# Hybrid encoder layer on one core: the mixers' weights split during the first feed-forward and kept in DRAM

## The chip, the core and the metric

One core of a Trainium2 chip runs the whole layer. The metric is the device time of one execution in microseconds; the median of three runs before the change is 1479.0 us (1477.66 to 1479.29).

## What is computed

One layer, on a prompt of 512 rows and a sample of 256 rows of width 1024, all in float32 (`rms_norm` scales by the root mean square of a row and by a gain):

```python
def encoder_layer(x, ...):
    x = x + 0.5 * swiglu(rms_norm(x, g_ffn1), w_ffn1_gu, w_ffn1_down)
    proj = rms_norm(x, g_mix) @ w_in            # 1024 x 3072
    a_q, a_k, a_v, b_q, b_k, b_v = split(proj)  # 512 columns each
    # mixer A: 8 heads x 64, dilated windows; mixer B: 4 heads, difference of two softmaxes
    # q and k: rms_norm per head, then rotary; outputs: rms_norm per head
    x = x + concat(norm(o_a), norm(o_b)) @ w_out  # 1024 x 1024
    x = x + 0.5 * swiglu(rms_norm(x, g_ffn2), w_ffn2_gu, w_ffn2_down)
    return rms_norm(x, g_final)
# swiglu: silu(g) * u @ w_down, g and u = halves of x @ w_gu, hidden width 2816
```

## The kernel before

**Precision.** Every float32 product is made of three: an operand is split into hi (rounded by a cast on ScalarE, ACT) and lo (the rest, a subtract on VectorE, DVE, or GpSimd, POOL), and hi x hi, hi x lo and lo x hi are summed in PSUM. A weight tile has both parts side by side and is 4 KB a partition for 128 x 512 values. `split3` (lines 253 to 256) makes this pair.

**Stages.** The first feed-forward (`f1`, about 31 to 534 us), the mixers (about 533 to 861 us), the output product through `w_out` (about 860 to 947 us) and the second feed-forward (`f2`). The 768 rows are six tiles of 128. 

**Feed-forward.** The hidden width is 22 chunks of 128. A chunk's gate and up products use seven products instead of eight by sums of weight blocks (Strassen's scheme as Winograd arranged it): POOL makes the sums S1 to S4, ACT and DVE split seven weight tiles. Chunks come in groups (3, 3, 3, 3, 3, 2, 2, 3); after each group but the last, its down products run, into six PSUM banks, one a row tile, in `contract` (line 148), first for column half 0, then for half 1. `run` (line 373) lists steps of two functions, a preparation (loads and splits) and a run (matmuls and evictions); the preparation is traced `AHEAD = 3` steps before its run. With the first two chunks done in `begin`, `f1` has 20 x 7 product steps, 19 x 2 down steps, 6 preparations for the last group, 6 row tiles and one step of its own for the rotary tables, 191 in all. Weight pairs live in `ws` (6 buffers), raw tiles in `sf` (3) and `blk`.

**Order.** The program is traced in this order, and a scheduler that works with modelled times then fixes each engine's instruction order; each engine, and the SP queue that issues nearly all DMAs, runs strictly in it.

**Mixers.** Eight units: 0 to 3 are mixer B's heads, 4 to 7 pairs of mixer A's heads. Twelve `quantum` slots a unit project it from the normalized rows: half a row tile each, 12 matmuls of 384 columns with `ws` as the moving operand (line 644). `rotary` normalizes q and k (r_z is a step of the root, line 84), rotates them on POOL (lines 668, 669) and DVE (line 675, qd); `scores`, `transposed` (line 745, pT) and `values` (line 761) are attention, 13 slots behind. A unit's weights come in four pieces kk of 256 rows x 384 columns: `load_piece` (line 612) loads a raw tile in two DMAs, casts it on ACT (line 620) and subtracts on POOL (line 621) into one of five `ws` buffers. Piece 0 is asked for five slots ahead, pieces 1 and 2 one slot ahead, piece 3 at the unit's first slot. `raw` has two buffers. Mixed outputs of units 0 to 5 go to DRAM (`mT_dram`, line 813).

**Output product.** From slot 98, `early_out` multiplies the mixed tiles 0 to 5 (`mTs`, fetched back by `mixed_split`, line 866, through the same `raw` buffers) with 24 pieces of `w_out` (`early_piece`, line 872: load, ACT cast, POOL subtract). Units 6 and 7 follow with four pieces that `f2.half` (line 272) loads and splits.

Of the kernel before, what the change touches and what calls it, by code (L numbers as in the profile page):

```python
# [10 lines left out]
F32 = mybir.dt.float32  # L11
F32R = mybir.dt.float32r
# [23 lines left out]
def encoder_layer(ctx: ExitStack, tc: tile.TileContext, a, y_prompt, y_sample):  # L36
    nc = tc.nc
    V, S, G, T = nc.vector, nc.scalar, nc.gpsimd, nc.tensor
    dma = nc.sync.dma_start
# [4 lines left out]
    dpool = ctx.enter_context(tc.tile_pool(name="dram", bufs=1, space=bass.MemoryType.DRAM))  # L44
# [27 lines left out]
    xp = XPool()  # L72
# [180 lines left out]
    def split3(dst, src, lo=V):  # L253
        hi = S.copy(dst[:, 0], src)  # L254
        lo.tensor_tensor(dst[:, 1], src, dst[:, 0].bitcast(F32), op=ALU.subtract)  # L255
        return hi

    class FeedForward:
# [111 lines left out]
                for k, t in enumerate(self.tmp):  # L370
                    split3(self.B[nm][k], t[:, slot])

        def run(self, tail, aside=None):

            steps = []
            act = self.act
# [148 lines left out]
        V.tensor_scalar(gcol[:, 28:29], gcol[:, 28:29], 1.0 - LAMBDA_INIT, None, op0=ALU.mult)  # L525


    tabs = tc.alloc_tile_pool(name="tabs", bufs=1, reuse_waits="tile")
    with tile_pool(name="h1", bufs=12) as h1, tile_pool(name="b1", bufs=7) as b1, tile_pool(name="w1", bufs=6) as w1:
        made = []  # L530

        def hb1(name):
            n = len(made)
            if n < 16:
                if n % 2 == 0:
                    made.append(hpool.tile([P, 2, 2, HALF], F32R, tag="blk", name=name))
# [16 lines left out]
        f1.begin(lambda: three_rows((3, 4, 5), third, "n1b", (V, V, None)), lambda: rows_between((0, 1, 2), third, "n1a"),  # L553
                 True)
        hT2 = []

        def post1(t, n):
            if n == 0:
                if len(later) >= 3:
                    run_later()  # L560
                return
            if t == 0:
                roots_table()
                hT2.extend(hpool.tile([P, 2, NTOK], F32R, tag="blk", name=f"hTb{k}") for k in range(KT))
# [18 lines left out]
    with tile_pool(name="w2", bufs=5) as w2, tile_pool(name="mix", bufs=2) as mp:  # L583
        nbias = mp.tile([P, 896], F32, tag="nbias", name="nbias", bufs=1)
        dma(nbias, a["nbias"])

        lst = w2.tile([P, 768], F32, tag="raw", name="lam_st", bufs=2)
        l4 = lst[:, 0:256].rearrange("p (a b d) -> p a b d", b=2, d=64)
        for i, nm in enumerate(("lam_q1", "lam_k1", "lam_q2", "lam_k2")):
            dma(l4[:, i // 2, i % 2, :], row_of(nm))  # L590
# [9 lines left out]
        state = {}  # L600
# [9 lines left out]
            return bass.AP(ap.tensor, ap.offset + step, [*outer, (-step, two), inner])  # L610

        def load_piece(u, kk):
            base = 0 if is_a(u) else 1536
            w3 = w_in[:, base:base + 1536].rearrange("(k p) (s c) -> p k s c", p=P, s=3)
            raw = w2.tile([P, 2, 3, P], F32, tag="raw", name=f"wi{u}_raw{kk}", bufs=2)
            for e in range(2):
                dma(raw[:, e], w3[:, kk * 2 + e, :, (u % 4) * P:(u % 4 + 1) * P])
            s = w2.tile([P, 2, 2, 384], F32R, tag="ws", name=f"wi{u}_ws{kk}", bufs=5)
            rr = raw.rearrange("p k s c -> p k (s c)")
            S.copy(s[:, 0], rr)  # L620
            G.tensor_tensor(s[:, 1], rr, s[:, 0].bitcast(F32), op=ALU.subtract)  # L621
# [113 lines left out]
        def transposed(u, si, m, qt):  # L735
            nt = SEQS[si][1]
            nm = f"a{u}s{si}_{m}{qt}"
            pt = state["sm", u, si, m if is_a(u) else 0, qt]
            e = qt % 2
            if e == 0:  # L740
                state["pT", u, si, m, qt // 2] = mp.tile([P, 2, nt, 256], F32R, tag="pT", name=f"{nm}_pT")
            dst = state["pT", u, si, m, qt // 2]
            ps = bank([P, nt, P], f"{nm}_tp")
            for k in range(nt):
                T.transpose(ps[:, k, :], pt[:, k * P:(k + 1) * P], ident)
            split(dst[:, 0, :, e * P:(e + 1) * P], dst[:, 1, :, e * P:(e + 1) * P], ps)
# [81 lines left out]
        for u in range(8):  # L828
# [4 lines left out]
            n = s0  # L833
# [30 lines left out]
        early = {}  # L864

        def mixed_split(u):
            raw = w2.tile([P, NTOK], F32, tag="raw", name=f"mTraw{u}", bufs=2)
            dma(raw, mT_dram[u])
            mTs[u] = hpool.tile([P, 2, NTOK], F32R, tag="blk", name=f"mTs{u}")
            split(mTs[u][:, 0], mTs[u][:, 1], raw)  # L870

        def early_piece(c, n):
            raw = w2.tile([P, 512], F32, tag="raw", name=f"eo{c}{n}_raw", bufs=2)
            dma(raw, w_out[rows_of(c), n * 512:(n + 1) * 512])
            ws = w2.tile([P, 2, 512], F32R, tag="ws", name=f"eo{c}{n}_ws", bufs=5)
# [16 lines left out]
        for i in range(24):  # L892
            c, n, g = i % 6, i // 6 % 2, i // 12
# [11 lines left out]
    with tile_pool(name="h3", bufs=28) as h3, tile_pool(name="w3", bufs=6) as w3:  # L905
        wt3 = w_tiles(w3)
        f2 = FeedForward("f2", a["w_ffn2_gu"], a["w_ffn2_down"], 16,
                         lambda name: h3.tile([P, 2, HALF], F32R, tag="hb", name=name),
                         lambda shape, dtype, name: hpool.tile(shape, dtype, tag="blk", name=name), wt3,
                         (4, 4, 4, 4, 3, 3))  # L910
        third = lambda name: wt3([P, D], F32, "gf", name)


        wo = {(c, n): f2.half(w_out, (c + 4) % 8, n, f"wo{c}{n}") for c in (6, 7) for n in range(2)}
        for tiles in ((3, 4, 5), (0, 1, 2)):
            for t in tiles:
                for n in range(2):
# [78 lines left out]
```

## Time and profile before

| | |
|---|---|
| median of three runs | 1479.0 us (1477.66 to 1479.29) |
| the profiled execution: its own time | 1477.56 us |
| its span, first to last instruction | 1475.7 us |
| PE (matmul) busy | 1441.2 us |
| DVE, ACT, POOL busy | 1080.0, 675.5, 441.9 us |
| DMA moved | 103.06 MB |

A busy PE is not PE at its peak, since matmuls are pipelined; where it idles, the wait views name the engine that ended the idle time. [...] Instructions are named out<-in by the program's tile names with the numbers left out, after line and engine; SPq is the SP queue's issue of a DMA. Times are us from the span's start.

### The profile page before, as it was taken

The numbers are of one execution on the slowest core, as the hardware profiler recorded it, in microseconds if no ns is written. First come the engines' busy times: TensorE is split into PE (matmuls) and PEld (weight loads), VectorE is DVE, ScalarE is ACT, GpSimd is POOL, SyncE is SP. The second block draws the span as 40 slices with busy tenths as digits, with TensorE's granted clock in tenths as the row PEclk, the third lists the DMA queues.
The fourth block names the chain that finished last, engine by engine and source line by source line (L and its number), as shares of the span: only waits on it lengthen the run. The fifth ranks groups of instructions, "written<-read, shape, count | busy, mean of one in ns | idle before, by whom it ended". The sixth has DMA issues, their size and how long they took to land.

```text
span 1475.7 us, 21779 instructions
## 1 busy us (share of the span) xinstructions
PE 1441.2 (98%) x8041; PEld 1349.7 (91%) x8041; DVE 1080.0 (73%) x1983; ACT 675.5 (46%) x1471; POOL 441.9 (30%) x323
## 2 busy tenths in 40 slices
PE   6999999999999999999999999999999999999997
PEld 6989999998999999999999987899898999989895
DVE  6867676676777777888887885797584865847586
ACT  6423233332333466666677775553241332414245
POOL 3253213131223224443433234232232312222222
PEclk9999999999999999999999999999999999999999
DMA  4322121213221211111111034123132131312212
GB/s 143 104 64 86 43 87 43 86 46 98 83 75 43 80 56 44 51 47 54 55 47 41 30 101 140 53 72 100 43 94 64 44 100 44 100 58 63 81 43 86
DMA packets 141667, 103.06 MB, mean 70 GB/s; under 512 B 7133, under 2 KB 122618, under 8 KB 141562
## 3 DMA queue, kind: packets, MB, share of 16 engines
q1 hardware_dynamic: 141504, 101.67, 22.4%
q8 instruction: 63, 1.03, 0.3%
q14 instruction: 42, 0.34, 0.1%
q10 hardware_dynamic: 58, 0.01, 0.0%
HBM read 96.16 MB, written 5.51 MB: 69 GB/s over the span
## 4 chain that ended last, share of the span: by engine, by line
PE 76%; DVE 10%; ACT 4%; DMA 3%; POOL 3%; issue 2%; SPq 0%; POOLq 0%; ACTq 0%; DVEq 0%
PE f_p L198 40%; PE f_n0t L148 11%; PE f_n1t L148 11%; PE f L311 3%; DMA wi_raw<-in_w_in 1%; DMA eo_raw<-in_w_out 1%; PE u6s0b_pj L644 1%; PE u7s0b_pj L644 1%; POOL wi_ws L621 1%; POOL eo_ws L877 1%; PE f_y L148 1%; DVE x L153 1%; DVE hTb L122 1%; PE eo_t5n L148 1%; PE eo_t4n L148 1%
## 5 line engine op out<-in xcount | busy, mean ns | idle before, releaser
L198 PE MATMUL f_p<-f_bT,f_wS 128*128 128x384 f32 x1440 | 257.4, 335 | 0.0
L198 PEld LDWEIGHTS f_p<-f_bT,f_wS 128*128 128x128 f32 x1440 | 251.5, 188 | 0.0
L254 ACT CAST f_wS<-f_S 128x512 fp32r<-128x512 f32 x160 | 99.2, 621 | 299.4 <-PE f_n1t L148 125.4
L176 POOL TENSOR_TENSOR f_S<-f_raw,f_S 128x512 f32<-128x512 f32 x40 | 62.3, 1558 | 405.1 <-DVE f_wS L255 405.1
L198 PE MATMUL f_p<-f_b,f_wA 128*128 128x384 f32 x960 | 173.1, 335 | 0.0
L198 PEld LDWEIGHTS f_p<-f_b,f_wA 128*128 128x128 f32 x960 | 167.4, 188 | 1.0
L255 DVE TENSOR_TENSOR f_wS<-f_S,f_wS 128x512 fp32r<-128x512 f32 x160 | 124.1, 791 | 57.2 <-ACT f_wS L254 57.2
L148 PE MATMUL f_n0t<-f_d_ws,f_act 128*128 128x512 f32 x684 | 159.9, 392 | 0.0
L148 PE MATMUL f_n1t<-f_d_ws,f_act 128*128 128x512 f32 x684 | 159.6, 392 | 0.0
L148 PEld LDWEIGHTS f_n1t<-f_d_ws,f_act 128*128 128x128 f32 x684 | 128.3, 188 | 29.0
L148 PEld LDWEIGHTS f_n0t<-f_d_ws,f_act 128*128 128x128 f32 x684 | 128.1, 188 | 28.3
L255 DVE TENSOR_TENSOR f_wA<-f_raw,f_wA 128x512 fp32r<-128x512 f32 x136 | 115.8, 871 | 29.3 <-ACT f_wA L254 29.0
L254 ACT CAST f_wA<-f_raw 128x512 fp32r<-128x512 f32 x136 | 82.1, 620 | 73.2 <-PE f_n0t L148 58.2
L176 POOL TENSOR_TENSOR f_S<-f_raw 128x512 f32<-128x512 f32 x40 | 55.8, 1396 | 161.0 <-DVE f_d_ws L255 127.7
L254 ACT CAST f_d_ws<-f_d_raw 128x512 fp32r<-128x512 f32 x88 | 54.7, 622 | 101.9 <-PE f_p L198 60.4
L198 PE MATMUL f_p<-f_bT,f_wA 128*128 128x384 f32 x480 | 90.5, 335 | 0.0
L198 PE MATMUL f_p<-f_b,f_wS 128*128 128x384 f32 x480 | 90.2, 335 | 0.0
L206 DVE TENSOR_TENSOR f_ev<-f_p,f_u 128x384 f32<-128x384 f32 x120 | 66.5, 554 | 31.5 <-PE f_p L198 31.4
L198 PEld LDWEIGHTS f_p<-f_bT,f_wA 128*128 128x128 f32 x480 | 84.3, 188 | 0.0
L198 PEld LDWEIGHTS f_p<-f_b,f_wS 128*128 128x128 f32 x480 | 84.1, 188 | 0.0
L255 DVE TENSOR_TENSOR f_d_ws<-f_d_raw,f_d_ws 128x512 fp32r<-128x512 f32 x88 | 62.7, 713 | 26.5 <-ACT f_d_ws L254 21.8
L621 POOL TENSOR_TENSOR wi_ws<-wi_raw,wi_ws 128x768 fp32r<-128x768 f32 x32 | 58.9, 1848 | 59.0 <-ACT wi_ws L620 56.6
(911 smaller groups left out, 2783.4 us busy)
## 6 DMA issues: line engine op xcount, KB each, us to landing
f_raw<-in_w_ffn_gu SPq DMA_DIRECT2D x88, 512.0 KB, 3.9
f_d_raw<-in_w_ffn_down SPq DMA_DIRECT2D x88, 256.0 KB, 3.0
wi_raw<-in_w_in SPq DMA_DIRECT2D x64, 192.0 KB, 2.6
eo_raw<-in_w_out SPq DMA_DIRECT2D x24, 256.0 KB, 2.6
mTraw<-mT_dram SPq DMA_DIRECT2D x6, 384.0 KB, 2.9
x<-in_x_prompt SPq DMA_DIRECT2D x4, 512.0 KB, 5.8
y_prompt<-nf_o SPq DMA_DIRECT2D x8, 256.0 KB, 2.3
x<-in_x_sample SPq DMA_DIRECT2D x2, 512.0 KB, 5.4
```

The lines of the kernel that those rows point to most:

```text
L122: V.scalar_tensor_tensor(lo, ps[:, k - k0], gc, hi.bitcast(F32), op0=ALU.mult, op1=ALU.subtract)
L148: T.matmul(ps, lhs[:, ll, t * P:(t + 1) * P], ws[:, rl, off:off + cols], start=(first and ll == 0 and rl == 0), stop=(last and ll == 1))
L153: V.scalar_tensor_tensor(xs, ps, scale, xs, op0=ALU.mult, op1=ALU.add)
L176: G.tensor_tensor(q[nm], q[x], q[y], op=op)
L198: T.matmul(ps, w[:, wl, k * P:(k + 1) * P], self.ff.B[bn][k][:, xl, :], start=(k == 0 and wl == 0 and xl == 0), stop=(k == HK - 1 and wl = ...
L206: V.tensor_tensor(dst, self.ps[nm], other, op=ALU.add)
L254: hi = S.copy(dst[:, 0], src)
L255: lo.tensor_tensor(dst[:, 1], src, dst[:, 0].bitcast(F32), op=ALU.subtract)
L311: T.matmul(p, w[:, wl, k * P:(k + 1) * P], self.B[bn[j]][k][:, xl, :], start=(j == 0 and k == 0 and wl == 0 and xl == 0), stop=(j == 1 and ...
L621: G.tensor_tensor(s[:, 1], rr, s[:, 0].bitcast(F32), op=ALU.subtract)
L644: T.matmul(ps, hT2[k][:, xl, tok:tok + P], w[:, wl, k % 2, :], start=(k == 0 and xl == 0 and wl == 0), stop=(k == KT - 1 and xl == 1))
L877: G.tensor_tensor(ws[:, 1], raw, ws[:, 0].bitcast(F32), op=ALU.subtract)
```

## The change

During `f1`'s run, all of `w_in` (48 pieces of 128 x 512) and `w_out` (16 such pieces) are loaded, split by `split3` (ACT cast, DVE subtract) and stored to DRAM tiles `wi_dram` and `wo_dram`, in which a row of 4 KB holds hi and lo of one partition. The store of a piece is issued together with the next piece's split. The raw tile uses the single `junk` buffer, the pair one of the two `xn` buffers. The steps are inserted into the list of `run`; they have no preparation.

In the mixers `load_piece` issues four DMAs straight into `ws` (hi and lo, two blocks of 128 rows each); `early_piece` and the four last pieces of `w_out` issue one DMA. Cast and subtract go. `raw` has one buffer instead of two, `pT` three instead of two.

```diff
+    def fetch_ahead(i):
+        waiting["raw"] = xp.tile([P, 512], F32, "junk", f"sa{i}_raw")
+        dma(waiting["raw"], pieces[i][0])
+    def split_ahead(i):
+        if "ws" in waiting:
+            ws, dst = waiting.pop("ws")
+            dma(dst, ws.bitcast(F32))
+        if i < len(pieces):
+            ws = xp.tile([P, 2, 512], F32R, "xn", f"sa{i}_ws")
+            split3(ws, waiting["raw"])
+            waiting["ws"] = ws, pieces[i][1]
+    ahead = [e for i in range(len(pieces)) for e in ((i + 0.3, lambda i=i: fetch_ahead(i)),
+                                                     (i + 1.0, lambda i=i: split_ahead(i)))]
+    ahead.append((len(pieces) + 1.0, lambda: split_ahead(len(pieces))))
...
+            if spread:
+                rate = (len(steps) - 30) / spread[-1][0]
+                for when, fn in reversed(spread):
+                    steps.insert(6 + int(when * rate), (lambda: None, fn))
...
-        f1.run(post1, prepare)
+        f1.run(post1, prepare, ahead)
...
         def load_piece(u, kk):
-            raw = w2.tile([P, 2, 3, P], F32, tag="raw", name=f"wi{u}_raw{kk}", bufs=2)
+            s = w2.tile([P, 2, 2, 384], F32R, tag="ws", name=f"wi{u}_ws{kk}", bufs=5)
+            c = u % 4 * P
             for e in range(2):
-                dma(raw[:, e], w3[:, kk * 2 + e, :, (u % 4) * P:(u % 4 + 1) * P])
-            s = w2.tile([P, 2, 2, 384], F32R, tag="ws", name=f"wi{u}_ws{kk}", bufs=5)
-            S.copy(s[:, 0], rr)
-            G.tensor_tensor(s[:, 1], rr, s[:, 0].bitcast(F32), op=ALU.subtract)
+                for l in range(2):
+                    dma(s[:, l, e].bitcast(F32).rearrange("p (s c) -> p s c", c=P),
+                        wi_dram[u // 4, kk * 2 + e, :, :, l, c:c + P].rearrange("s p c -> p s c"))
...
-                state["pT", u, si, m, qt // 2] = mp.tile([P, 2, nt, 256], F32R, tag="pT", name=f"{nm}_pT")
+                state["pT", u, si, m, qt // 2] = mp.tile([P, 2, nt, 256], F32R, tag="pT", name=f"{nm}_pT", bufs=3)
...
-            raw = w2.tile([P, NTOK], F32, tag="raw", name=f"mTraw{u}", bufs=2)
+            raw = w2.tile([P, NTOK], F32, tag="raw", name=f"mTraw{u}", bufs=1)
...
         def early_piece(c, n):
-            raw = w2.tile([P, 512], F32, tag="raw", name=f"eo{c}{n}_raw", bufs=2)
-            dma(raw, w_out[rows_of(c), n * 512:(n + 1) * 512])
             ws = w2.tile([P, 2, 512], F32R, tag="ws", name=f"eo{c}{n}_ws", bufs=5)
-            S.copy(ws[:, 0], raw)
-            G.tensor_tensor(ws[:, 1], raw, ws[:, 0].bitcast(F32), op=ALU.subtract)
+            dma(ws.bitcast(F32), wo_dram[(c + 4) % 8, n])
...
-        wo = {(c, n): f2.half(w_out, (c + 4) % 8, n, f"wo{c}{n}") for c in (6, 7) for n in range(2)}
+                wo[c, n] = wt3([P, 2, 512], F32R, "ws", f"wo{c}{n}")
+                dma(wo[c, n].bitcast(F32), wo_dram[(c + 4) % 8, n])
```

## Rows read from the trace of the kernel before

**Rows 1.** The page, busy time of each engine (share of span, instructions).

```profile
PE 1441.2 (98%) x8041; PEld 1349.7 (91%) x8041; DVE 1080.0 (73%) x1983; ACT 675.5 (46%) x1471; POOL 441.9 (30%) x323
```

**Rows 2.** Busy times by stretch: length, PE, PEld, DVE, ACT, POOL, clock, DMA, GB/s.

```profile
95.87:139.90 44.03, 44.03 (x253) 44.03 (x253) 34.98 (x51) 18.15 (x32) 11.65 (x9) 1.00 0.28 84
139.90:164.42 24.52, 24.52 (x109) 20.27 (x109) 13.48 (x19) 4.56 (x7) 6.17 (x5) 1.00 0.15 43
...
618.00:659.00 41.00, 39.59 (x271) 38.96 (x270) 35.08 (x90) 27.28 (x78) 16.05 (x10) 1.00 0.16 49
...
741.00:782.00 41.00, 41.00 (x289) 40.44 (x288) 33.13 (x89) 30.23 (x81) 14.84 (x10) 1.00 0.16 49
```

**Rows 3.** PE's waits, 577 to 741 us: who for whom, total us, times, longest.

```profile
PE a0s_o L761 <- DVE a1s_p L733: 1.4, 1, 1.4
PE a1s_o L761 <- DVE a2s_p L733: 1.4, 1, 1.4
PE a2s_o L761 <- DVE a3s_p L733: 1.3, 1, 1.3
PE a3s_o L761 <- ACT a3s_pT L90: 0.7, 1, 0.7
```

**Rows 4.** Timeline (start, length, engine, line) of DVE and POOL in units 2 to 4.

```profile
618.23 0.15 DVE L84 TENSOR_TENSOR u2s0b_r_z<-u2s0b_r_y 128x8 f32<-128x8 f32 x1
...
643.95 1.84 POOL L621 TENSOR_TENSOR wi_ws<-wi_raw,wi_ws 128x768 fp32r<-128x768 f32 x1 [2.31 <-ACT wi_ws L620]
644.46 1.35 DVE L84 TENSOR_TENSOR u2s1b_r_z<-u2s1b_r_y 128x8 f32<-128x8 f32 x1
...
647.76 2.32 DVE L675 TENSOR_TENSOR u2s1b_qd<-u2s1b_qn,tb_S 128x512 f32<-128x512 f32 x1 [0.89 <-POOL u2s1b_qn L668]
...
702.75 1.70 DVE L675 TENSOR_TENSOR u4s0b_qd<-u4s0b_qn,ta_S 128x512 f32<-128x512 f32 x1
```

**Rows 5.** Timeline of PE and busy times with the clock, end of the mixers.

```profile
856.67 0.51 PE L761 MATMUL a6s_o<-a6s_pT,u6s1b_v 128*128 128x256 f32 x2 [0.81 <-DVE a6s_pT L91]
...
857.40:860.90 3.50, 3.50 (x16) 3.40 (x17) 2.48 (x10) 3.06 (x7) 0.96 (x1) 0.51 0.56 185
...
902.12 0.39 PE L761 MATMUL a7s_o<-a7s_pT,u7s1b_v 128*128 128x256 f32 x1 [1.48 <-ACT a7s_pT L90]
```

**Rows 6.** Instruction group of POOL's subtracts: count, busy us, mean ns, idle before.

```profile
L621 POOL TENSOR_TENSOR wi_ws<-wi_raw,wi_ws 128x768 fp32r<-128x768 f32 x32 | 58.9, 1848 | 59.0 <-ACT wi_ws L620 56.6 <-PE a5s_o L761 2.3
```

**Rows 7.** The page, DMA issues: count, KB each, median us to landing.

```profile
wi_raw<-in_w_in SPq DMA_DIRECT2D x64, 192.0 KB, 2.6
```

**Rows 8.** Timeline of PE, POOL and SP where unit 4 follows unit 3.

```profile
676.19 1.72 PE L644 MATMUL u3s1b_pj<-wi_ws,hTb 128*128 128x384 f32 x9
...
678.95 3.69 POOL L621 TENSOR_TENSOR wi_ws<-wi_raw,wi_ws 128x768 fp32r<-128x768 f32 x2 [2.65 <-ACT wi_ws L620]
...
680.86 2.71 SPq L617 DMA_DIRECT2D wi_raw<-in_w_in  x4
...
681.62 0.85 PE L644 MATMUL u4s0b_pj<-wi_ws,hTb 128*128 128x384 f32 x4
```

**Rows 9.** Timeline of the mixed tiles: fetches, first split, one output product.

```profile
847.54 0.96 DVE L91 TENSOR_TENSOR mTs<-mTraw,mTs 128x768 fp32r<-128x768 f32 x1 [0.28 <-ACT mTs L90]
...
862.94 0.32 SPq L868 DMA_DIRECT2D mTraw<-mT_dram  x1
...
869.42 0.32 SPq L868 DMA_DIRECT2D mTraw<-mT_dram  x1
...
878.06 0.50 PE L148 MATMUL eo_t0n<-eo_ws,mTs 128*128 128x512 f32 x1
```

**Rows 10.** Weight splits of the first feed-forward (group, timeline) and a first use.

```profile
L255 DVE TENSOR_TENSOR f_wS<-f_S,f_wS 128x512 fp32r<-128x512 f32 x9 | 7.1, 805 | 0.0
...
130.41 0.68 DVE L255 TENSOR_TENSOR f_d_ws<-f_d_raw,f_d_ws 128x512 fp32r<-128x512 f32 x1
...
139.74 1.08 PE L148 MATMUL f_n0t<-f_d_ws,f_act 128*128 128x512 f32 x4
```

More of the change, by code (lines that the diff above doesn't have):

```diff
@@ L371, in begin, with run @@
                     split3(self.B[nm][k], t[:, slot])
-        def run(self, tail, aside=None):
+        def run(self, tail, aside=None, spread=()):
             steps = []
@@ L525, in gains @@
         V.tensor_scalar(gcol[:, 28:29], gcol[:, 28:29], 1.0 - LAMBDA_INIT, None, op0=ALU.mult)
+    wi_dram = dpool.tile([2, KT, 3, P, 2, 512], F32, tag="wid", name="wi_dram")
+    wo_dram = dpool.tile([8, 2, P, 2, 512], F32, tag="wod", name="wo_dram")
+    w_in, w_out = a["w_in"], a["w_out"]
+    pieces = [(w_in[k * P:(k + 1) * P, (1 - m) * 1536 + s * 512:(1 - m) * 1536 + (s + 1) * 512], wi_dram[m, k, s])
+              for m in range(2) for k in range(KT) for s in range(3)]
+    pieces += [(w_out[c * P:(c + 1) * P, n * 512:(n + 1) * 512], wo_dram[c, n]) for c in range(8) for n in range(2)]
+    waiting = {}
+    def fetch_ahead(i):
[12 more added lines that the diff above has]
+    ahead.append((len(pieces) + 1.0, lambda: split_ahead(len(pieces))))
     tabs = tc.alloc_tile_pool(name="tabs", bufs=1, reuse_waits="tile")
@@ L571, in prepare @@
             tab["B"] = tables(wt1, "g_b_q", "g_b_k", "tb")
-        f1.run(post1, prepare)
-    w_in, w_out = a["w_in"], a["w_out"]
+        f1.run(post1, prepare, ahead)
     is_a = lambda u: u >= 4
@@ L585, in encoder_layer @@
         dma(nbias, a["nbias"])
-        lst = w2.tile([P, 768], F32, tag="raw", name="lam_st", bufs=2)
+        lst = w2.tile([P, 768], F32, tag="raw", name="lam_st", bufs=1)
         l4 = lst[:, 0:256].rearrange("p (a b d) -> p a b d", b=2, d=64)
@@ L612, in load_piece @@
         def load_piece(u, kk):
-            base = 0 if is_a(u) else 1536
-            w3 = w_in[:, base:base + 1536].rearrange("(k p) (s c) -> p k s c", p=P, s=3)
-            raw = w2.tile([P, 2, 3, P], F32, tag="raw", name=f"wi{u}_raw{kk}", bufs=2)
+            s = w2.tile([P, 2, 2, 384], F32R, tag="ws", name=f"wi{u}_ws{kk}", bufs=5)
+            c = u % 4 * P
             for e in range(2):
-                dma(raw[:, e], w3[:, kk * 2 + e, :, (u % 4) * P:(u % 4 + 1) * P])
-            s = w2.tile([P, 2, 2, 384], F32R, tag="ws", name=f"wi{u}_ws{kk}", bufs=5)
-            rr = raw.rearrange("p k s c -> p k (s c)")
-            S.copy(s[:, 0], rr)
-            G.tensor_tensor(s[:, 1], rr, s[:, 0].bitcast(F32), op=ALU.subtract)
+                for l in range(2):
+                    dma(s[:, l, e].bitcast(F32).rearrange("p (s c) -> p s c", c=P),
+                        wi_dram[u // 4, kk * 2 + e, :, :, l, c:c + P].rearrange("s p c -> p s c"))
             state["w", u, kk] = s
@@ L911, in encoder_layer @@
         third = lambda name: wt3([P, D], F32, "gf", name)
-        wo = {(c, n): f2.half(w_out, (c + 4) % 8, n, f"wo{c}{n}") for c in (6, 7) for n in range(2)}
+        wo = {}
+        for c in (6, 7):
+            for n in range(2):
+                wo[c, n] = wt3([P, 2, 512], F32R, "ws", f"wo{c}{n}")
+                dma(wo[c, n].bitcast(F32), wo_dram[(c + 4) % 8, n])
         for tiles in ((3, 4, 5), (0, 1, 2)):
```

## The prediction

> **What bounds the kernel now.** I read the page's busy line first: the matrix engine PE is busy for 1441.2 of 1475.7 us [rows 1]. Nothing but PE's own idle time, or work taken off PE, can move the end, and the change takes no matmul away. So the question is where PE waits. The busy times by stage come next [rows 2]: in a three-chunk product phase of the first feed-forward, and in the down-projection after it, PE has no idle time at all; in the mixers a 41 us stretch of the B units has PE busy for 39.59, and one of the A units for 41.00. The waits of PE from 577 to 741 us name what is missing in the B units: four waits of the value product, 1.4 + 1.4 + 1.3 + 0.7 = 4.8 us [rows 3], behind VectorE (DVE) and ScalarE (ACT). Next, DVE around one of these waits [rows 4]: the tiny r_z multiply of eight columns takes 1.35 us while POOL is in its weight subtract (643.95 for 1.84 us), and 0.15 us where POOL is idle; the rotary product qd takes 2.32 us under the next weight subtract and 1.70 us beside POOL's own rotary work. That is 1.20 + 0.62 = 1.82 us lost on DVE, more than the longest wait of PE that follows it. Last, the end of the mixers [rows 5]: PE waits 0.8 us before 861 us, its granted clock is 0.51 for 3.5 us right after, and it waits 1.5 us once more at about 902 us.
>
> **What is taken away.** Of the mixers' 32 unit pieces POOL loses all subtracts, 58.9 us [rows 6], and ACT the cast in front of each; the 24 early output pieces go the same way. None of it is on PE, so its length is worth nothing by itself. Its worth is the hold that POOL's subtract has on DVE. Without it the 1.82 us come back at each of the four places, more than each wait: I put all 4.8 us [rows 3] to the gain. Bounds: 0, if another wait of the same length stands behind it, and 4.8. I take the upper end, since the A units, with the same attention chain and 33 us of DVE instead of 35, run at 41.00 of 41 [rows 2]. A third buffer for pT also loosens that chain; I give it nothing of its own.
>
> [...]
>
> **End of the mixers.** At 846 to 861 us the cast and subtract of the first output pieces stand between attention's last steps on ACT and POOL. [...] But attention's latency itself stays, on DVE. Between 0 and 4.0 us I take half, 2.0 us.
>
> **What is added in the first feed-forward.** There are 64 pieces (48 of w_in, 16 of w_out), each one load, an ACT cast, a DVE subtract and a store of 512 KB. The step list has 191 steps, so a piece comes every (191 - 30) / 65 = 2.48 steps. A product step is 44.03 / 21 = 2.10 us, so a three-chunk phase takes 8.5 pieces; a down step is 24.52 / 6 = 4.09 us, so a down phase takes 2.4 [rows 2]. A DVE subtract of this size is 0.68 us with POOL quiet and 0.805 us on average in such a phase [rows 10]. DVE then has 34.98 + 8.5 x 0.805 = 41.8 of 44.03 us: 95%, not over. In the down phase it has 13.48 + 1.9 of 24.52, so a lag can be made up there. ACT, at 18.15 of 44.03, has ample room. What covers PE is the lead of the weights: a down weight is split at 130.41 + 0.68 = 131.09 us and first multiplied at 139.74 us, 8.65 us later [rows 10]. I cost this edit at 0. If the cover is gone, the price is that of the slower rival below. The empty preparation steps thin the three-step lookahead in the listing to about two real steps, but the lead just shown is set by buffers, not by it.
>
> On the SP queue each piece adds a load and a store. The store comes with the next split, 2.48 steps after its own, so SP should find it ready; were it not, the loads of the feed-forward would be queued behind it, and these have the 8.65 us lead. The DMA engines carry 0.28 of their time in a product phase [rows 2]; three quarters of a megabyte more every 5.2 us is 151 GB/s, on top of 84 GB/s at a share of 0.28, hence at most 0.28 x 235 / 84 = 0.78 at the same packet efficiency. Loads land later, by up to about one store, but not at the path.
>
> **Unit loads.** The loads now write straight into ws, four per piece, and must wait for a ws buffer instead of a raw one. Unit 4 shows the room: piece 1 takes the buffer of unit 3's piece 0, which the row at 676.19 still reads for 0.7 us or so; unit 4 starts at 681.62 and comes to its piece 1 after six of its matmuls, at about 682.8 [rows 8]. Before, POOL finished that piece at 678.95 + 1.84 = 680.8 us [rows 8], 2.0 us early. Four issues at 2.71 / 4 = 0.68 us at the most (waits within that row counted) put the last at 677.0 + 2.0 = 679.0, and a landing of 2.6 us [rows 7] ends at 681.6: 1.2 us early. The old chain was longer for the later pieces (piece 2's subtract ends at 682.64, piece 3's comes after it), so these gain. I cost this at 0; bound upward in a rival. The mT store that stands ahead of them on SP waits for ACT, as it does now.
>
> **The single raw buffer.** Mixed tiles are now fetched one at a time. Before, fetches stood 869.42 - 862.94 = 6.48 us apart [rows 9]. This is the second rival. The four last w_out pieces lose cast and split ahead of 930 us, where PE has other work: 0.
>
> **Sum.** 4.8 + 2.0 = 6.8 us less. The profiled execution took 1477.56 us (span 1475.7 and 1.9 around it): 1470.8. The median shown is 1.44 us above it, so 1472.2 us.
>
> **Rivals.**
> *Slower: DVE falls behind in the first feed-forward.* DVE's free 9.05 us of a product phase are waits for PE between evictions, not one block. If half of them can't be used, each three-chunk phase is 8.5 x 0.805 - 4.5 = 2.3 us over; 20 chunks make 6.7 phases, 15.6 us, hence 1472.2 + 15.6 = 1487.8. It decides once the lag within a phase eats the 8.65 us lead and the two spare PSUM banks. Against it: a deficit of 2.3 us is a quarter of the lead, and the down phase has 9 us free to pay it. For it: DVE order is fixed beforehand, with waits between.
> [...]
>
> *Mixed tiles late.* The first split ends at 848.5; five more rounds of fetch and split at 6.48 us end at 880.9, while the sixth is multiplied at 878.06 now [rows 9]: 2.8 us back, 1475.0. Against it: ACT and POOL are relieved there, so the period should shrink.
>
> *Nothing comes of it.* Either the next wait takes the place of the one removed (DVE stays at about 34 of 41), or unit loads land late: with a landing 2 us longer than 2.6 us, piece 1 is 0.8 us late in seven units, 5.6 us, and most of the gain is gone. 1477 to 1479.
>
> **How the numbers follow.** Forecast with its own spread, 1466 to 1474: 0.60. Mixed tiles late, about 1475.0: 0.13. Nothing comes of it: 0.13. Slower: 0.14. Faster is the first two, 0.73. Within 0.2% (about 3 us, what a measurement of this kernel can tell from no change) 0.13; slower 0.14. The range runs from 1465.5 (all 8.8 us of waits and clock gone, and some 5 us of smaller holds of POOL on DVE elsewhere in the mixers) up to 1482.5, about a third of the slower rival's price.
>
> **What would show it.** Right: product phases still 44.03 us long with DVE at 41 to 43 us; r_z at 0.15 us in every unit; PE's waits in the B units below 1 us in sum; 41 us from unit to unit down to about 39.6; granted clock 1.00 near 857 us. Wrong: PE waits for f_wS or f_wA in the first feed-forward, or product phases longer than 44.1; PE waits for a DMA at the first matmuls of a unit; PE waits for mTs between 861 and 885 us.

## The result: 57 us slower, and all of it in the first feed-forward

The changed kernel takes 1535.9 us (median of five runs, 1534.26 to 1538.56), the kernel before 1478.51 us (median of five, 1477.66 to 1479.29): a ratio of 1.0388, 95% interval 1.0376 to 1.0399. The profiled execution spans 1532.5 us, against 1475.7 before. Its busy line, beside [rows 1]:

```profile
PE 1464.9 (96%) x8041; PEld 1359.8 (89%) x8041; DVE 1090.4 (71%) x2043; ACT 675.4 (44%) x1475; POOL 350.2 (23%) x267
```

POOL has lost 91.7 us of work, the unit subtracts of [rows 6] and the output pieces' among them, and PE is idle for 67.6 us where it was for 34.5.

**Where it went.** Three marks split the span: the first product of the tile step that ends the first feed-forward, and the first projections of units 1 and 5. The first mark as a timeline shows it (start, length, engine, line), before and after:

```profile
505.38 2.01 PE L148 MATMUL f_y<-f_d_ws,f_act 128*128 128x512 f32 x8
```

```profile
567.30 2.92 PE L148 MATMUL f_y<-f_d_ws,f_act 128*128 128x512 f32 x12
```

This mark comes 61.9 us late. From unit 1 to unit 5 (559.3 to 722.7 before, 621.0 to 779.1 after) 5.3 us are won. The rest, from unit 5 to the end, is 753.0 before and 753.4 after. So 61.9 - 0.2 (the stretch to unit 1) - 5.3 + 0.4 = 56.8 us.

**The mixers did what the prediction said.** Busy times by stretch, from unit 1 to unit 5, before and after (columns as in [rows 2]):

```profile
559.30:722.70 163.40, 158.85 (x1072) 156.23 (x1071) 135.39 (x335) 107.77 (x301) 66.98 (x42) 1.00 0.16 47
```

```profile
621.00:779.10 158.10, 158.10 (x1071) 156.29 (x1070) 126.70 (x335) 97.30 (x283) 34.87 (x24) 1.00 0.35 97
```

PE has no idle time left here, so the waits of [rows 3] are gone, and DVE does the same 335 instructions in 8.7 us less. The r_z and qd of [rows 4], which took 1.35 and 2.32 us, are now (duration in ns: least, median, most):

```profile
L84 DVE TENSOR_TENSOR u2s1b_r_z<-u2s1b_r_y x1: 149/149/149, 702.3 to 702.3; 128x8 f32<-128x8 f32 x1
...
L703 DVE TENSOR_TENSOR u2s1b_qd<-u2s1b_qn,tb_S x1: 692/692/692, 704.5 to 704.5; 128x512 f32<-128x512 f32 x1
```

**The first feed-forward.** A fixed stretch of it, before and after, and then of after the product phase and the down phase that answer to [rows 2], and two short stretches behind a wait of PE:

```profile
60.00:460.00 400.00, 400.00 (x2088) 373.29 (x2087) 280.75 (x410) 131.30 (x225) 110.41 (x92) 1.00 0.24 71
```

```profile
60.00:460.00 400.00, 363.33 (x1784) 327.63 (x1783) 272.07 (x405) 145.50 (x255) 99.00 (x85) 0.96 0.56 182
...
100.17:152.43 52.26, 46.82 (x253) 45.05 (x252) 38.40 (x59) 21.26 (x38) 12.82 (x9) 0.97 0.61 198
152.43:184.15 31.72, 26.96 (x109) 21.20 (x109) 18.56 (x27) 9.05 (x16) 4.84 (x3) 0.95 0.57 196
117.50:120.90 3.40, 3.40 (x10) 2.99 (x11) 3.30 (x6) 1.08 (x2) 1.95 (x2) 0.53 0.25 98
...
247.40:254.20 6.80, 5.36 (x14) 3.87 (x13) 4.09 (x3) 1.39 (x3) 2.94 (x2) 0.50 0.38 142
```

The phases of 44.03 and 24.52 us take 52.26 and 31.72. PE idles for 36.7 of 400 us, and the granted clock, 0.96 of full speed in the mean (before: 1.00), costs some 0.04 x 400 = 16 us more by estimate: after several of PE's longer waits it stands at about half, as from 117.5 us on, where it is 0.53 for 3.4 us, or from 247.4 us on, 0.50 for 6.8 us. No engine is full: DVE, which the slower rival was about, is busy for 38.40 of 52.26 us, and the DMA engines for 0.61. What PE waits for from 60 to 430 us (total, times, longest; before it waited for nothing there):

```profile
PE f_p L198 <- ACT f_wA L254: 17.5, 8, 3.8
PE f_n0t L148 <- ACT f_act L254: 6.5, 3, 2.5
PE f_n0t L148 <- DVE f_act L255: 5.7, 4, 1.6
PE f_p L198 <- DVE f_wS L255: 4.0, 5, 1.4
PE f_n1t L148 <- DVE x L153: 2.2, 3, 1.0
```

The same view for the engines behind them, of the pieces' own steps alone:

```profile
ACT sa_ws L254 <- DMA sa_raw<-in_w_in: 78.1, 30, 5.2
DVE sa_ws L255 <- ACT sa_ws L254: 62.0, 37, 3.8
ACT sa_ws L254 <- DMA sa_raw<-in_w_out: 27.1, 10, 5.3
...
SPq L544 <- DVE sa_ws L255: 90.9, 48, 4.5
SPq L544 <- DMA sa_raw<-in_w_in: 75.4, 35, 4.2
```

The prediction had no counterpart of these rows. A piece's raw tile has one buffer, so the chain is a ring: the fetch waits on SP for the fetch and the subtract of the piece before, the cast on ACT for the fetch to land, the subtract on DVE for the cast. On all three the feed-forward's own instructions are queued behind these waits. Two of PE's stalls in the timeline of after, from the queue to PE (in brackets the idle time before the instruction, and what ended it):

```profile
109.16 0.33 SPq L544 DMA_DIRECT2D sa_raw<-in_w_in  x1
...
110.02 1.75 SPq L166 DMA_DIRECT2D f_raw<-in_w_ffn_gu  x2
...
112.26 0.62 ACT L254 CAST sa_ws<-sa_raw 128x512 fp32r<-128x512 f32 x1 [1.20 <-DMA sa_raw<-in_w_in]
116.82 1.14 ACT L254 CAST f_wA<-f_raw 128x512 fp32r<-128x512 f32 x2 [3.94 <-DMA f_raw<-in_w_ffn_gu]
...
117.49 1.42 PE L198 MATMUL f_p<-f_b,f_wA 128*128 128x384 f32 x3 [2.49 <-ACT f_wA L254]
...
152.44 0.38 SPq L544 DMA_DIRECT2D sa_raw<-in_w_in  x1
...
153.35 1.58 SPq L274 DMA_DIRECT2D f_d_raw<-in_w_ffn_down  x2
...
157.59 0.62 ACT L254 CAST f_d_ws<-f_d_raw 128x512 fp32r<-128x512 f32 x1 [4.45 <-DMA f_d_raw<-in_w_ffn_down]
...
158.25 0.69 DVE L255 TENSOR_TENSOR f_d_ws<-f_d_raw,f_d_ws 128x512 fp32r<-128x512 f32 x1 [3.45 <-ACT f_d_ws L254]
...
163.30 0.73 PE L148 MATMUL f_n0t<-f_d_ws,f_act 128*128 128x512 f32 x2 [2.50 <-ACT f_act L254]
```

In the first, the two f_raw loads of chunk 4 stand on SP behind the fetches and stores of nine pieces. They go out at 110.02 us, the first lands at about 116.8, and its cast, done at once, ends a wait of PE of 2.49 us. Before the change the same loads left SP as their buffers came free, the first at 76.82 us, and those of the next chunk behind them up to 100.2 (four loads in one row):

```profile
76.82 23.79 SPq L166 DMA_DIRECT2D f_raw<-in_w_ffn_gu  x4
```

In the second stall, a load for the down products is late in the same way; ACT and DVE stand still for it, and the act tile that PE needs is behind them.

### The profile page after: what moved, and what is told of

Same layout as the page of the kernel before. It is cut to its first block, busy times and chain, and to the rows that moved or that the text cites. A ratio compares the mean times of both kernels' runs of the same rounds, so it can differ in the third digit from the quotient of the medians.

```text
span 1532.5 us, 22029 instructions
## 1 busy us (share of the span) xinstructions
PE 1464.9 (96%) x8041; PEld 1359.8 (89%) x8041; DVE 1090.4 (71%) x2043; ACT 675.4 (44%) x1475; POOL 350.2 (23%) x267
## 4 chain that ended last, share of the span: by engine, by line
PE 70%; DMA 10%; DVE 6%; ACT 2%; issue 1%; POOL 1%; SPq 0%; ACTq 0%; DVEq 0%; POOLq 0%
PE f_p L198 27%; PE f_n1t L148 7%; PE f_n0t L148 7%; DMA f_raw<-in_w_ffn_gu 3%; DMA sa_raw<-in_w_in 3%; PE f_y L148 2%; PE f L311 2%; DMA sa_raw<-in_w_out 2%; DMA f_d_raw<-in_w_ffn_down 1%; DVE sa_ws L255 1%; PE u7s0b_pj L672 1%; PE u4s0b_pj L672 1%; PE u1s0b_pj L672 1%; PE u0s0b_pj L672 1%; PE u6s0b_pj L672 1%; PE u3s0b_pj L672 1%
## 5 line engine op out<-in xcount | busy, mean ns | idle before, releaser
L198 PE MATMUL f_p<-f_b,f_wA 128*128 128x384 f32 x960 | 184.6, 348 | 19.8 <-ACT f_wA L254 19.2
L198 PEld LDWEIGHTS f_p<-f_b,f_wA 128*128 128x128 f32 x960 | 174.3, 196 | 26.7 <-ACT f_wA L254 22.3
L148 PE MATMUL f_n0t<-f_d_ws,f_act 128*128 128x512 f32 x684 | 167.4, 403 | 12.2 <-ACT f_act L254 6.5
L148 PEld LDWEIGHTS f_n0t<-f_d_ws,f_act 128*128 128x128 f32 x684 | 131.4, 193 | 44.8 <-ACT f_act L254 8.1
L255 DVE TENSOR_TENSOR f_wS<-f_S,f_wS 128x512 fp32r<-128x512 f32 x160 | 128.3, 815 | 48.6 <-ACT f_wS L254 48.6
L255 DVE TENSOR_TENSOR f_wA<-f_raw,f_wA 128x512 fp32r<-128x512 f32 x136 | 110.3, 829 | 46.4 <-ACT f_wA L254 46.3
L255 DVE TENSOR_TENSOR sa_ws<-sa_raw,sa_ws 128x512 fp32r<-128x512 f32 x64 | 52.6, 822 | 62.8 <-ACT sa_ws L254 62.0
L254 ACT CAST sa_ws<-sa_raw 128x512 fp32r<-128x512 f32 x64 | 39.8, 621 | 123.1 <-DMA sa_raw<-in_w_in 83.2
```

Source lines behind the costliest of these rows:

```text
L148: T.matmul(ps, lhs[:, ll, t * P:(t + 1) * P], ws[:, rl, off:off + cols], start=(first and ll == 0 and rl == 0), stop=(last and ll == 1))
L198: T.matmul(ps, w[:, wl, k * P:(k + 1) * P], self.ff.B[bn][k][:, xl, :], start=(k == 0 and wl == 0 and xl == 0), stop=(k == HK - 1 and wl = ...
```

## Experiments

"f1" below is by how much the mark f_y comes later than in the kernel before (505.4 us), "units" the length from unit 1 to unit 5 (163.4 before), "rest" what follows (753.0), each of the profiled run. The runs are from three chips: the kernel before, run beside them, has a median of 1478.6 us for e1 to e4, 1478.9 for e5 to e8, 1478.0 for e9 and e10, and 1480.7 for e11 and e12. The ratios below go by these medians. The three stretches are of one execution each, against one trace of the kernel before.

| run | f1 | units | rest | median, us |
|---|---|---|---|---|
| changed kernel | +61.9 | 158.1 | 753.4 | 1535.9 |
| e1 four pieces | +3.3 | 158.3 | 752.3 | 1474.8 |
| e2 no stores | +26.2 | 159.0 | 753.7 | 1499.5 |
| e3 splits alone | +10.7 | 157.8 | 751.5 | 1481.3 |
| e4 POOL's queue | +49.0 | 158.3 | 753.4 | 1523.1 |
| e5 traffic alone | +4.5 | 159.0 | 754.0 | 1478.2 |
| e6 program order | +31.6 | 158.2 | 753.6 | 1505.0 |
| e7 three raws | +21.3 | 158.3 | 753.8 | 1493.5 |
| e8 lookahead | +65.5 | 158.4 | 751.1 | 1536.6 |
| e9 uncoupled | +10.5 | 157.9 | 751.6 | 1481.6 |
| e10 uncoupled, POOL subtracts | +8.3 | 158.6 | 751.9 | 1481.3 |
| e11 B-units only | +2.4 | 159.3 | 757.0 | 1479.5 |
| e12 B-units, POOL subtracts | +3.6 | 159.6 | 758.4 | 1481.5 |

The first four were to tell three theories apart: order on SP's queue, traffic, and the work on ACT and DVE.

**e1: four pieces.**

```diff
-    ahead = [e for i in range(len(pieces)) for e in ((i + 0.3, lambda i=i: fetch_ahead(i)),
+    ahead = [e for i in (0, 1, 2, 48) for e in ((i + 0.3, lambda i=i: fetch_ahead(i)),
...
-                        wi_dram[u // 4, kk * 2 + e, :, :, l, c:c + P].rearrange("s p c -> p s c"))
+                        wi_dram[0, 0, :, :, l, c:c + P].rearrange("s p c -> p s c"))
...
-            dma(ws.bitcast(F32), wo_dram[(c + 4) % 8, n])
+            dma(ws.bitcast(F32), wo_dram[0, 0])
```

> Only 4 of the 64 pieces (three of w_in, one of w_out) are split ahead and stored; the mixers and the output projection load these four for every unit and row, in the same sizes and runs as in the changed kernel, so the products use wrong weights. The first feed-forward is then nearly that of before, the mixers are those of the changed kernel. If all of the loss lies in the first feed-forward, as the excess of TensorE's start-to-start times in the two traces says (about 58 us lost there, about 10 us won in the mixers): 1466 to 1471 us. If the loads of four parts in the mixers cost as much as the split on POOL and ACT did, or the 10 us is an accident of the profiled run: 1476 to 1481 us.

1474.8 us, a ratio of 0.9976 (0.9964 to 0.9987), between the two. The loss is all in the first feed-forward, and the mixers' gain is real: the units take 158.3 us. But the four pieces still cost 3.3 us at the start, and of the end only 0.7 us come back.

**e2: no stores.** As e1 in the mixers; all pieces are fetched and split, four stored.

```diff
-            dma(dst, ws.bitcast(F32))
+            if dst in kept:
+                dma(kept[dst], ws.bitcast(F32))
```

> All 64 pieces are fetched and split during the first feed-forward, but only 4 of them stored; the mixers load these four everywhere, so the products use wrong weights. The 64 fetches keep their place on SP's queue: seven stand in a row ahead of the loads of chunk 4, each waiting for VectorE's subtract of the piece before. The added traffic falls from 50 MB to 18 MB. Theory 1 (the loads of the feed-forward stand on SP behind that chain): at least half of the loss in the first feed-forward stays, 1500 to 1530 us. Theory 2 (traffic: loads land late because the DMA engines are shared with 64 KB-row stores): a third of the loss stays, 1483 to 1492 us. Theory 3 (64 casts on ACT and 64 subtracts on VectorE): nothing changes, 1530 to 1540 us.

1499.5 us, 1.0142 (1.0122 to 1.0162): just under what theory 1 expected, above theory 2, and far from 3. (The "64 KB-row stores" are a slip; a stored row has 4 KB.) Fetches and their waits remain (ACT waits 85.0 + 33.2 us for them, not less than in the changed kernel), yet no wait of PE for f_wA is left. So in this chain the stores make the difference between a late load that is still covered and one that is not, but they are not the whole.

**e3: splits alone.**

```diff
     def fetch_ahead(i):
+        if i:
+            return
```

On top of e2; every split reads the one fetched tile.

> One piece is fetched; the 64 casts and 64 subtracts all work on it, and 4 results are stored; the mixers load these four everywhere, so the products use wrong weights. ACT and VectorE have all of the change's work, SP and the DMA engines almost none of it. Theory 1 (order on SP's queue) and theory 2 (traffic): the first feed-forward is as before, 1466 to 1473 us. Theory 3 (the work on ACT and VectorE, the slower rival of the prediction): most of the loss stays, 1515 to 1540 us.

1481.3 us, 1.002 (1.001 to 1.0031): neither. 64 casts and subtracts cost 10.7 - 3.3 = 7.4 us in the first feed-forward. That is the slower rival's mechanism, at half of its price of 15.6 us. With no fetch to wait for, the splits are bunched here: all 64 casts run between 32 and 161 us. Its stretch, with PE busy for 395.64 us and DVE for 310.27, 29.5 more than before:

```profile
60.00:460.00 400.00, 395.64 (x2055) 368.36 (x2056) 310.27 (x457) 159.68 (x279) 120.13 (x92) 1.00 0.24 72
```

**e4: POOL's queue.**

```diff
-        dma(waiting["raw"], pieces[i][0])
+        nc.gpsimd.dma_start(waiting["raw"], pieces[i][0])
...
-            dma(dst, ws.bitcast(F32))
+            nc.gpsimd.dma_start(dst, ws.bitcast(F32))
```

> The changed kernel in full, but the 64 fetches and 64 stores are issued by POOL instead of SP; nothing is left out. Traffic and splits are the same; SP's order of the feed-forward's loads is that of before. Theory 1 (order on SP): the feed-forward's loads are early again, 1466 to 1480 us, with some of POOL's sums a little later. Theory 2 (traffic): 1525 to 1540 us. Theory 3 (ACT and VectorE): 1525 to 1540 us.

1523.1 us, 1.0301 (1.0281 to 1.0322). Theory 1 alone fails: SP's order is that of before, PE waits for f_wA no more, and 49.0 of the 61.9 us stay. The ring has only moved. Its waits from 60 to 560 us (engine, for whom, total, times, longest):

```profile
POOL sa_raw L544 <- DVE sa_ws L255: 180.0, 54, 7.8
ACT sa_ws L254 <- DMA sa_raw<-in_w_in: 119.7, 36, 6.4
DVE sa_ws L255 <- ACT sa_ws L254: 95.3, 40, 5.0
```

ACT and DVE wait longer than in the changed kernel (78.1 and 62.0), and PE now waits 16.8 us for ACT's f_act. The traffic is as it was with SP as the issuer: 184 GB/s at a DMA share of 0.56 from 60 to 460 us, against 182 and 0.56 in the changed kernel. And f_raw lands about as late: it takes a median of 6.2 us from 60 to 430 us, 6.6 in the changed kernel and 3.8 before.

So a fourth theory, A: the waits themselves, on every in-order queue that the ring passes, and not the order of one queue, the bytes or the work. Against it B, the traffic. The next four separate these.

**e5: traffic alone.** One split, whose tile is stored for every piece; fetches and stores in program order on SP (`keep_in_program_order` keeps an instruction at its place in the listing).

```diff
...
-        if i < len(pieces):
+        if i == 0:
             ws = xp.tile([P, 2, 512], F32R, "xn", f"sa{i}_ws")
```

> The split of 63 of the 64 pieces is left out: every piece is fetched and 512 KB are stored for every piece, but always the first split piece, so the mixers' weights are wrong. Fetches and stores are held in program order on SP, which spreads them over the whole first feed-forward. SP and the DMA engines carry all of the added 50 MB; ACT and VectorE do nothing for it, and no fetch waits for VectorE. Theory A (the in-order queues: ACT waits for a fetched piece, VectorE for ACT's cast, SP for VectorE's subtract, with the feed-forward's own work queued behind): nearly all of the loss is gone, 1473 to 1480 us. Theory B (traffic: the feed-forward's 512 KB loads land 6.4 us after issue in the changed kernel where before they took 3.8 us): half or more of the loss stays, 1500 to 1530 us.

1478.2 us, 0.999 (0.9978 to 1.0001). Theory B falls. Busy times from 60 to 460 us, and the loads' landing from 60 to 430 us (KB each, median us from issue):

```profile
60.00:460.00 400.00, 396.76 (x2071) 369.86 (x2070) 276.54 (x403) 129.25 (x226) 111.31 (x90) 1.00 0.58 193
```

```profile
f_raw<-in_w_ffn_gu SPq DMA_DIRECT2D x30, 512.0 KB, 6.5
```

The DMA engines carry more than in the changed kernel (193 against 182 GB/s), and f_raw lands as late, 6.5 us after its issue against

```profile
f_raw<-in_w_ffn_gu SPq DMA_DIRECT2D x28, 512.0 KB, 6.6
```

in the changed kernel. But ACT and DVE have no step in the ring, ACT waits for no f_raw (28.1 us in the changed kernel), and PE is idle for 3.2 us. This run is not free of waits: SP waits 111.2 us for the fetch before to land, and ACT 40.7 us for f_d_raw (29.5 in the changed kernel). So neither the traffic, with a landing 2.7 us longer, nor waits on SP alone make the loss.

**e6: program order.** The changed kernel with its fetches and stores in program order on SP:

```diff
-        dma(waiting["raw"], pieces[i][0])
+        tc.keep_in_program_order(dma(waiting["raw"], pieces[i][0]))
...
-            dma(dst, ws.bitcast(F32))
+            tc.keep_in_program_order(dma(dst, ws.bitcast(F32)))
```

> The changed kernel in full, with its fetches and stores held in program order on SP: on SP the pieces then stand at most four in a row (seven in the changed kernel) and spread over the whole first feed-forward. Same splits, same traffic at a slower pace. Theory A (in-order queues behind the chain of one raw buffer): the chain has more time for each piece, so a third to two thirds of the 61 us go, 1495 to 1515 us. Theory B (traffic): the added rate falls by about a fifth, and the loss with it, 1520 to 1530 us. Nothing at all, 1530 to 1540 us, if neither the order on SP nor the pace matters.

1505.0 us, 1.0173 (1.0143 to 1.0202), as theory A had it: half of the loss goes, with the same work and the same bytes. PE waits for f_wA no more. ACT still waits 80.4 + 14.6 us for fetches (60 to 460 us), and PE for ACT and DVE behind it. SP waits longer for the subtracts than in the changed kernel, 137.7 us against 90.9 (60 to 430 us), so their length alone is not the price.

**e7: three raw buffers.**

```diff
-        waiting["raw"] = xp.tile([P, 512], F32, "junk", f"sa{i}_raw")
+        sr = pools["sr"]
+        waiting["raw"] = sr.tile([P, 512], F32, tag="sr", name=f"sa{i}_raw") if i % 3 else xp.tile([P, 512], F32, "junk", f"sa{i}_raw")
```

> The changed kernel in full, with three raw buffers for the fetches in the place of one; nothing else is changed. A fetch then waits for the subtract three pieces earlier, so it can land before ACT comes to its cast. Theory A (in-order queues): ACT's 105 us of waits for fetched pieces go, and with them more than half of the loss, 1485 to 1505 us. Theory B (traffic): the pieces come faster and so does the traffic, 1525 to 1545 us.

1493.5 us, 1.0095 (1.0066 to 1.0125), as theory A had it: 40.6 of the 61.9 us go by one change of a size. That is what the single buffer cost here, on a ring that is off the path. The fetches now follow each other every 3.1 us at the median (5.0 in the changed kernel), and the next buffer of the ring is the limit, the two split tiles that the stores still read:

```profile
ACT sa_ws L254 <- DMA wi_dram<-sa_ws: 39.9, 24, 4.3
```

The denser traffic speaks against theory B once more. From 60 to 260 us, in this run:

```profile
60.00:260.00 200.00, 190.94 (x955) 171.99 (x954) 158.48 (x236) 90.02 (x158) 57.12 (x54) 0.98 0.84 285
```

PE idles for 9.1 us at 285 GB/s; in the changed kernel it idles for 20.9 us of the same stretch at 201 GB/s.

**e8: lookahead.**

```diff
-                    steps.insert(6 + int(when * rate), (lambda: None, fn))
+                    at_ = 6 + int(when * rate)
+                    prep_, run_ = steps[at_]
+                    steps[at_] = (prep_, lambda run_=run_, fn=fn: (fn(), run_()))
```

> The changed kernel in full, but each piece rides on an existing step of the first feed-forward instead of a step of its own, so that the lookahead of three steps is again three real steps (in the changed kernel a piece's empty preparation takes the place of a real one, and it falls to about two). If the thinner lookahead is what makes the feed-forward's loads late: 1490 to 1515 us. If not (theories A and B): 1530 to 1540 us.

1536.6 us, 1.0386 (1.0356 to 1.0416). The thinner lookahead is not the cause, as the prediction said of it.

**e9: uncoupled.** Three raws, program order, and each fetch about two and a half pieces ahead of its split:

```diff
-    ahead = [e for i in range(len(pieces)) for e in ((i + 0.3, lambda i=i: fetch_ahead(i)),
+    ahead = [e for i in range(len(pieces)) for e in ((max(i - 1.7, 0.0), lambda i=i: fetch_ahead(i)),
```

> The changed kernel in full, with three raw buffers, each fetch placed some two and a half pieces ahead of its split, and fetches and stores held in program order on SP. No queue then has to wait for a step of the piece chain, at the slow pace that leaves the two split buffers time to drain. If the loss was those waits, what is left is the work itself (6.5 us for the splits by the run with splits alone) and the traffic (3.4 us by the run with traffic alone) against the 3.8 us won in the mixers: 1478 to 1486 us. If something else of the change costs (the mixture of traffic and splits): it stays where three raw buffers alone left it, 1490 to 1496 us.

1481.6 us, 1.0026 (1.0016 to 1.0036), with the same splits and 191 GB/s:

```profile
60.00:460.00 400.00, 394.19 (x2046) 365.87 (x2044) 300.60 (x459) 159.53 (x285) 110.17 (x90) 1.00 0.58 191
```

51.4 of the 61.9 us are gone, within the range expected if the loss was the waits, but not because no queue waits any more. SP waits for the ring twice as long as in the changed kernel, and ACT still waits, now for stores:

```profile
SPq L545 <- DVE sa_ws L255: 182.5, 37, 15.8
ACT sa_ws L254 <- DMA wi_dram<-sa_ws: 59.0, 20, 6.0
```

Most of these waits cost PE nothing. From 60 to 260 us it is idle for 0.05 us, with the splits and 189 GB/s beside it:

```profile
60.00:260.00 200.00, 199.95 (x1048) 186.78 (x1047) 152.14 (x231) 82.08 (x147) 63.19 (x58) 1.00 0.57 189
```

That the 10.5 us left are about the 10.7 of e3 does not make them the same loss: in e3 PE is idle for nothing from 165 to 460 us, when the splits are over, and here it loses only later. One of its two longest stalls here:

```profile
404.00 0.62 ACT L254 CAST sa_ws<-sa_raw 128x512 fp32r<-128x512 f32 x1 [6.10 <-DMA wo_dram<-sa_ws]
404.53 0.52 ACT L243 ACTIVATE f_ev<-f_ev 128x384 f32<-128x384 f32 x1
...
411.06 4.60 PE L148 MATMUL f_n0t<-f_d_ws,f_act 128*128 128x512 f32 x12 [2.41 <-ACT f_act L254]
```

ACT waits 6.10 us for a store, the feed-forward's f_ev stands behind that, and PE waits for the act tile made from it. So the sum of an engine's waits is not the price here; what stands behind each of them, and how near it is to its due time, is. How much of the 51.4 us belongs to SP, to ACT and to DVE the runs do not divide, and the earlier fetches were not run by themselves.

**e10: POOL subtracts.** As e9, with the pieces' lo part on POOL.

```diff
-            split3(ws, waiting.pop(("raw", i)))
+            split3(ws, waiting.pop(("raw", i)), G)
```

> As the run e9, and the 64 subtracts of the pieces go to POOL, which is the least busy of the three in the first feed-forward. If the 6.5 us of the splits alone are VectorE's queue (its 0.8 us subtract ahead of an add that TensorE waits for): 4 to 6 us less than e9, 1473 to 1480 us, which would be a version at or under the kernel before. If they are ACT's casts, or if POOL's slower subtract delays the sums of the weights: no better than e9, or worse by up to 5 us.

1481.3 us, 1.0022 (1.0012 to 1.0032): no better than e9. The first feed-forward is 2.2 us shorter in the profiled run, but the medians do not differ; that the 7.4 us are DVE's subtracts alone is not shown.

**e11 and e12: only the B-units' weights.** 24 pieces instead of 64; A-units and output product as before.

```diff
-              for m in range(2) for k in range(KT) for s in range(3)]
-    pieces += [(w_out[c * P:(c + 1) * P, n * 512:(n + 1) * 512], wo_dram[c, n]) for c in range(8) for n in range(2)]
+              for m in range(1) for k in range(KT) for s in range(3)]
```

> Nothing is left out. Only the 24 pieces of w_in that the B-units 0 to 3 read are split ahead (one about every 18 us, from the third chunk on, with the three raw buffers and the early fetches of e9); the A-units, the output projection and the buffers of the mixers are those of the kernel before. In the run with four pieces 5.1 us were won between the starts of units 1 and 5 (163.4 us before, 158.3 us there), 3.0 us lost at the start of the first feed-forward, and 0.7 us won in all that follows. If the win belongs to the B-units' weights: 158 to 160 us from unit 1 to unit 5, and with 24/64 of the 6.8 us of e9, 1474 to 1477 us, under the kernel before by 0.1 to 0.3%. If it needs the third pT buffer or the A-units' loads as well: 161 to 164 us there, 1477 to 1481 us.

> As e11, with the 24 subtracts on POOL. The two runs e9 and e10 do not differ by more than their scatter, so the same time as e11 within 1.5 us is expected; less by 1 to 3 us if VectorE's queue is what the pieces still cost in the first feed-forward.

e11 takes 1479.5 us against 1480.65, 0.999 (0.9981 to 0.9999), at the small end of what was expected; e12 1481.5 us, 1.0007 (0.9999 to 1.0016), 1.9 us more than e11, where at most 1.5 were expected. The B-units' own weights win 4.1 of the 5.3 us in the units (159.3 us), and the first feed-forward loses only 2.4 us. But the rest is 4.0 us longer than in the trace of the kernel before. Up to about 2 us of that may be the chip, on which the kernel before has a median of 1480.65 us instead of 1478.51. Beside that, PE's waits for the last pT tiles at the end of the mixers have grown:

```profile
PE a7s_o L801 <- ACT a7s_pT L90: 3.5, 2, 2.8
```

(1.5 us, once, before [rows 5]). ACT waits there for the raw output weights, 15.6 us in all against 9.7 before; why more was not followed. e11 is the one complete version whose interval lies below the kernel before, and it wins 1 us.

## Why the prediction was wrong

**What bounds the kernel:** right. No matmul goes away, only PE's waits and its clock count, and they are the loss.

**First term, 4.8 us at the B-units:** right; 5.3 us, and r_z and qd are shorter as described. In [rows 4] r_z ends at 644.46 + 1.35 = 645.81 us, with POOL's subtract (643.95 + 1.84 = 645.79). On qd more came back than the 0.62 us priced: it takes 0.692 us now, beside POOL's own rotary step too, where the prediction stopped at 1.70 (one qd of each of units 2 to 4 still takes 1.70 or 1.71). ACT's casts went with the same edit; no run takes either away alone. With POOL's subtract gone, r_z takes 0.149 us there, and at most 0.168 in any unit; by what way the subtract had held it no run shows.

**Second term, 2.0 us at the end of the mixers:** wrong; 0.7 in e1, and 0.4 lost in the changed kernel. No run shows the 4.0 us of which it is half: measured are waits of 0.8 and 1.5 us and a clock of 0.51 for 3.5 us [rows 5], and the 3.5 x 0.49 = 1.7 us for that clock are my estimate from them. Over the eleven runs with these mixers (the changed kernel to e10) the rest lies between 1.9 won and 1.0 lost, 0.2 won in the mean. In the changed kernel the rival "mixed tiles late" came true by another door. Timeline of after at the end of the mixers, and busy times with the clock right behind it:

```profile
904.65 0.38 SPq L896 DMA_DIRECT2D mTraw<-mT_dram  x1
...
911.62 0.83 ACT L90 CAST mTs<-mTraw 128x768 fp32r<-128x768 f32 x1 [3.03 <-DMA mTraw<-mT_dram]
912.36 0.58 ACT L719 CAST u7s0b_t<-u7s0b_qt 128x512 fp32r<-128x512 f32 x1
...
912.99 0.58 PE L737 MATMUL a7s_sc<-u7s0b_t,u7s0b_t 128*128 128x256 f32 x1 [3.07 <-ACT u7s0b_t L719]
```

```profile
915.50:919.00 3.50, 3.50 (x17) 3.40 (x17) 2.97 (x11) 2.88 (x7) 0.68 (x1) 0.50 0.09 33
```

I asked when the mixed tile is multiplied [rows 9]. The cost was not there: ACT waits 3.03 us for the single-buffered mTraw, the cast of u7s0b_t stands behind it, PE waits 3.07 us for that cast, and the clock falls to 0.50. The waits of [rows 5] were replaced by one of the same kind.

**Unit loads at 0, last w_out pieces at 0:** right. wi_ws lands 4.5 us after its issue (2.6 for wi_raw, [rows 7]), and PE waits for no unit's weights.

**The first feed-forward at 0:** this is the step that failed: put at 0, it lost 61.9 us, because the chain of a piece was priced by its busy time and its bytes, and its waits were put at nothing. Four sentences of it, one by one.

- "SP should find it ready." I asked this of the store alone, and SP waits for the split in front of a store only once, 5.5 us. The fetch in front of it has one raw buffer, so SP waits for DVE's subtract of the piece before: 90.9 us in 48 waits. The single `junk` buffer stood in the listing; who is queued behind that wait I never asked.
- "A piece comes every 2.48 steps." That is its place in the listing. The order on each queue is fixed when the kernel is built, and there nine pieces stand between the loads of chunks 3 and 4; the last fetch of all went out at 386 us, though the listing spreads them over nearly all steps of a stage that now ends after 567 us. In e6, held to the listing's order, half of the loss goes.
- "Loads land later, by up to about one store, but not at the path." The first half is right: 6.6 instead of 3.8 us, with a DMA share of 0.61 where I had 0.78 at most. The second half nearly holds where loads leave early (e5: 4.5 us lost in all), and fails where the fetches ahead have held them back.
- "The lead just shown is set by buffers, not by it." It was, before [rows 10]. The lead is no property of the buffers alone; it also needs a queue that issues as soon as a buffer is free (the first f_raw load of chunk 4 left SP at 76.82 us before, at 110.02 after). The waits of nine pieces in a row on that queue took it away.

The slower rival had the place and the sign, but not the mechanism: it priced DVE's 64 subtracts as work at 15.6 us. As work they cost, with the casts and bunched, 7.4 us (e3), and spread out beside the whole traffic next to nothing from 60 to 260 us (e9). The rest is PE's idle time, and the slower clock behind it, where SP, ACT or DVE stood still for the ring with something queued behind that PE needed soon; 51.4 of the 61.9 us go when the ring is loosened (e9). A count of busy time cannot show that: DVE was at 38.40 of 52.26 us when it was late. The range of the forecast ended at 1482.5 us, called about a third of this rival's price; from 1472.2 us on that is 10.3 us, two thirds.

## What to carry to other kernels

When work is moved into a stage "with room", write down for each of its instructions what it waits for and what is queued behind it on that engine; room in busy time was no cover for a wait here (ACT was busy for 21.26 of 52.26 us where PE waited 4.4 us for it). In this kernel a background chain of load, split and store with one raw buffer cost 61.9 us. Three buffers alone took back 40.6 of them; three buffers, fetches well ahead and fixed places on the queue 51.4. How long the chain's waits are in sum is no measure of their price: SP waits longer for it in e9 than in the changed kernel, 182.5 against 90.9 us. And loads that land 2.7 us later cost little here where their issue was early (e5, PE idle for 3.2 of 400 us).

## What was not expected of the hardware

The DMA engines carried 193 GB/s, 0.58 of their time, beside a matrix engine that lost 3.2 of 400 us (e5), and 285 GB/s, 0.84 of their time, beside one that was idle for 9.1 of 200 us (e7). A 512 KB load took 6.5 us instead of 3.8 in that company, and a 256 KB fetch in the same run 3.0. The granted clock made short waits dear: in the changed kernel it stood at about half for 3.4 us behind a wait of PE of 2.49 us, and for 6.8 us around waits of 2.04 and 1.44 us, while after one of 1.91 us, at 136.1 us, it stayed at 1.00. By the estimate above, 36.7 us of idle time from 60 to 460 us carried some 16 us more with them.
